# The first modulation columns from TensorE, and an affine step on ScalarE, in a two-block fp32 kernel

## The chip, the cores and the metric

One core of one Trainium2 chip runs the whole program. The metric is the device time of one execution in microseconds (us), the median of several runs. The engines are PE (TensorE; PEld is its weight load), DVE (VectorE), ACT (ScalarE), POOL (GpSimd) and SP (SyncE, which issues the DMAs here).

## The reference, cut to what matters

Two transformer-like blocks work on 512 tokens of 1024 channels in fp32. Only the very start of the first block is touched:

```python
mod = jax.nn.silu(c) @ w_ada[l] + b_ada[l]
shift1, scale1, gate1, shift2, scale2, gate2 = [m[:, None, :] for m in jnp.split(mod, 6, axis=-1)]
h = rms_norm(x, norm1_w[l]) * (1.0 + scale1) + shift1
proj = h @ w_in[l]
```

`c` is one row of 1024 numbers, `w_ada` is 1024 by 6144. Of the 48 columns of 128 outputs that `mod` has, column k is the shift and column 8 + k the scale of channel tile k (k = 0 to 7). What follows in the block (a state-space mixer, attention, a gated merge, an MLP) and the second block (a recurrence and latent attention) is as before.

## The kernel before

Channels lie on partitions, tokens along the free axis; a k tile is 128 channels by 512 tokens. Products in near-fp32 precision are made of three: each operand is split into a high part (fp32r, a copy on ACT) and a low part (the difference, on DVE or POOL), and `mm3` (L166) issues high by high, high by low, low by high. The profile gives these three lines as L168 to L170. `weight` (L143) loads a weight tile into the ring "wr" of four slots (DMA, L153), casts the high part on ACT (L156) and subtracts the low part on DVE or POOL by a counter (L159). `split` (L162) does the same for activations (L163 and L164).

The start runs like this. `setup` and `mod_setup` load the identity, the bias `b_ada` and the norms. `silu_c` (L328) loads c as one row, takes Tanh on ACT, multiplies on DVE, and spreads the row over 128 partitions with two native fp32 matmuls (L339) into `cs`, copied on ACT (L340). `norm1` (L346) loads x in four tiles, takes sums of squares on ACT (L293) with small steps on POOL, scales x on DVE (L356), transposes it tile by tile on PE (L362, 32 transposes) and copies eight tiles `xt` to SBUF on ACT (L365).

Then comes the k loop (L370). In each turn one of seven weight tiles is loaded and split (`FIRST`, while k < 7). `mod_tiles` (L252) loads two 512 KB tiles of `w_ada`, rows 8 + k and k, into the same ring "wr", and for each one DVE multiplies 128 x 1024 elements by `cs` and sums along the row into a column of `modc` (L257). DVE adds the bias (L377) and forms the gain column (L379), applies gain and shift to xt in place (L382), and the split of xt follows (ACT L163, POOL L164). With that k tile the products of four output tiles go on that have their weights. Those of the last three (`NX`) stand at k = 7 in the source. After the loop, the convolutions of the mixer begin (ACT L469, DVE L478); the dt product goes through a chain on DVE that ends in `av` (L436), which PE needs for a cumulative sum (L441).

The order on each engine is not that of the source. The framework under the kernel follows source order as a priority, and lets an instruction pass that it expects to be ready sooner. So products of the last three output tiles run from 37 us on in the trace. Slots of a ring (four in "wr", four banks in the PSUM pool "px") are given out in that order, and SP's queue, on which all these loads stand, serves its list in order: a load that waits for a slot holds up those behind it. `LO["start"]` and `PAD` are tuning constants: which weights' low parts go to POOL, and words of padding at the head of a stage's small tiles.

Of the kernel before, what the change touches and what calls it, by code (L numbers as in the profile page):

```python
# [6 lines left out]
F32 = mybir.dt.float32  # L7
F32R = mybir.dt.float32r
AF = mybir.ActivationFunctionType
ALU = mybir.AluOpType  # L10
# [7 lines left out]
NEG = -1.0e30  # L18
FIRST = [4, 5, 0, 1, -1, 2, 3]
NX = 3  # L20
NSSD = 19
NF = 14
NATT = 12
# [26 lines left out]
       "xb0": "gpsimd", "xb1": "vector", "rq0": "vector", "rq1": "vector", "rq2": "vector"}  # L50
AFF = [0, 2]
FB = [32, 0]
PAD = [0, 16, 56, 0, 32, 0, 32, 0, 0, 0, 56, 0, 48, 32, 0, 0, 0, 0, 0, 0]


def r32(ap):
# [3 lines left out]
class Build:  # L60
# [261 lines left out]
    def mod_setup(self):  # L322
# [2 lines left out]
        self.n1 = self.load("norm1_w", [128, 8])  # L325
        self.n2 = self.load("norm2_w", [128, 8])

    def silu_c(self):  # L328

        nc, a = self.nc, self.a  # L330
        c, th = [self.pool("wr").tile([128, 1024], F32, tag="wr", name=self.nm("c"))[0:1] for _ in range(2)]
        nc.sync.dma_start(out=c, in_=a["c"])
        nc.scalar.activation(out=th, in_=c, func=AF.Tanh, scale=0.5)
        nc.vector.scalar_tensor_tensor(out=c, in0=th, scalar=1.0, in1=c, op0=ALU.add, op1=ALU.mult)
        half = self.c([1, 128], "half")
        nc.vector.memset(half, 0.5)
        for i in range(2):
            p = self.ps()
            nc.tensor.matmul(p, lhsT=half, rhs=c[:, i * 512:i * 512 + 512], start=True, stop=True)  # L339
            nc.scalar.copy(out=self.cs[:, i * 512:i * 512 + 512], in_=p)  # L340
# [5 lines left out]
    def norm1(self):  # L346
        nc, a = self.nc, self.a
        rs = self.stats("r1")
        xb = self.big("x")
        xv = xb.rearrange("p a b -> p (a b)").rearrange("p (t d) -> p t d", t=NT)  # L350
        for t in range(NT):
            nc.sync.dma_start(out=xv[:, t], in_=a["x"][t])
        for t in range(NT):
            for b in range(2):
                self.half_stats(rs, xv[:, t, b * 512:b * 512 + 512], b, t)
            nc.vector.tensor_scalar(out=xv[:, t], in0=xv[:, t], scalar1=rs[2][:, t:t + 1], scalar2=None, op0=ALU.mult)  # L356
        self.g1 = self.c([128, 8], "g1")
        xts = []
        for k in range(8):
            p = self.ps()  # L360
            for t in range(NT):
                nc.tensor.transpose(out=p[:, t * 128:t * 128 + 128], in_=xv[:, t, k * 128:k * 128 + 128],  # L362
                                    identity=self.ident)
            xt = self.t("xt")
            nc.scalar.copy(out=xt, in_=p)  # L365
            xts.append(xt)
        n = len(FIRST)
        pss = [self.pm() if m < 4 else self.ps() for m in range(n)]
        ws = []
        for k in range(8):  # L370
            if k < n:
                i = FIRST[k]
                src = a["w_dt"][0] if i < 0 else a["w_xbc"][i if i < 4 else 16 + 4 * (i - 4)]
                ws.append(self.weight(src, own=k >= n - NX))
            self.mod_tiles([8 + k, k])
            j = slice(k, k + 9, 8)
            nc.vector.tensor_tensor(out=self.modc[:, j], in0=self.modc[:, j], in1=self.bada[:, j], op=ALU.add)  # L377
            g = self.g1[:, k:k + 1]
            nc.vector.scalar_tensor_tensor(out=g, in0=self.modc[:, 8 + k:9 + k], scalar=1.0, in1=self.n1[:, k:k + 1],  # L379
                                           op0=ALU.add, op1=ALU.mult)  # L380
            xt = xts[k]
            nc.vector.tensor_scalar(out=xt, in0=xt, scalar1=g, scalar2=self.modc[:, k:k + 1], op0=ALU.mult,  # L382
                                    op1=ALU.add)
            self.split(self.hh[:, k], self.hl[:, k], xt, eng=self.e("hsplit"))
            late = range(n - NX, n) if k == 7 else []
            for m, k1 in [(m, k1) for m in range(n - NX) for k1 in range(8) if max(m, k1) == k] + \
                    [(m, k1) for m in late for k1 in range(8)]:
                wh, wl = ws[m]
                self.mm3(pss[m][:wh.shape[2]], wh[:, k1], wl[:, k1], self.hh[:, k1], self.hl[:, k1], k1 == 0, k1 == 7)
        return pss  # L390
# [885 lines left out]
def emit(tc, a, out, dbg=None, stages=("b1", "b2")):  # L1276
    with ExitStack() as ctx:
        b = Build(tc, ctx, a, out, dbg)
        tail = ctx.enter_context(ExitStack())
        with b.phase(nw=NW), ExitStack() as inner:  # L1280
            b.setup()
            if "b1" in stages:
                b.mod_setup()
                with ExitStack() as A:
                    A.enter_context(b.phase(nbig=3))
                    b.cs = b.c([128, 1024], "cs")
                    cpool = b.pool("c")
                    big = lambda n, p=b.pool("big"): p.tile([128, 8, 512], F32R, tag="big", name=b.nm(n))
                    b.hh, b.hl, b.accS = b.big("hh", F32R), b.big("hl", F32R), b.big("accS")
                    with b.phase(nt=9, nbig=1, nx=2 * NX):  # L1290
                        b.lo_pool = LO["start"]
                        b.silu_c()
                        first = b.norm1()
                        b.cpool = cpool
                        b.ssd_setup()
                        b.cpool = None
                    A.enter_context(b.phase(nf=NF))
                    with b.phase(nt=NSSD):
                        b.lo_pool = LO["ssd"]
                        b.ssd(first)  # L1300
                    O = A.enter_context(ExitStack())
                    O.enter_context(b.phase(nbig=2))
                    b.oh, b.ol = b.big("oh", F32R), b.big("ol", F32R)
                    with b.phase(nt=NATT):
                        b.lo_pool = LO["attn"]
                        b.attention()
                    tail.enter_context(b.phase(nbig=1, side="right"))
                    b.lo_pool = LO["merge"]
                    b.residual_setup()
                    G = ExitStack()  # L1310
                    G.enter_context(b.phase(nt=3, side="right"))
                    b.gb = {j: b.c([128, 1024], f"gb{j}") for j in (16, 40)}
                    b.mh, b.ml = big("mh"), big("ml")
                    with b.fills():
                        b.merge()
                    b.mod_cols(16, 32)
                    b.gate_rows(16, 0.5)
                    b.gate_rows(40, 1.0)
                    b.out_proj()
# [30 lines left out]
def pack(i):  # L1350
# [4 lines left out]
    i = {k: np.asarray(v) for k, v in i.items()}  # L1355
    o = {}

    def cm(w):
        k, m = w.shape
        return w.reshape(k // 128, 128, m // 128, 128).transpose(2, 1, 0, 3)  # L1360
# [5 lines left out]
    def col(v):  # L1366
        return v.reshape(-1, 128).T

    o["x"] = i["x"].reshape(4, 128, 1024)
    o["c"] = i["c"].reshape(1, 1024)  # L1370
    o["w_ada"] = i["w_ada"][0].T.reshape(48, 128, 1024)
    o["b_ada"] = col(i["b_ada"][0])
    o["norm1_w"], o["norm2_w"] = col(i["norm1_w"][0]), col(i["norm2_w"][0])
# [87 lines left out]
```

## Time and profile before

| | us |
|---|---|
| median of 3 runs | 1675.04 (1671.86 to 1677.4) |
| the profiled execution | 1674.92 |
| its span, first to last instruction | 1673.1 |
| PE busy | 1591.9 (95%) |
| DVE busy | 1130.0 (68%) |
| ACT busy | 784.3 (47%) |
| POOL busy | 447.4 (27%) |

The profile is of one execution. Busy times are sums over an engine's instructions; a matmul's end is modelled, so that a busy PE may still have room. The rows in the section further down name a line of the kernel, an engine, the operation, the tiles written and read, and where an engine stood idle before, what released it.

### The profile page before, as it was taken

The numbers are of one execution on the slowest core, as the hardware profiler recorded it, in microseconds if no ns is written. First come the engines' busy times: TensorE is split into PE (matmuls) and PEld (weight loads), VectorE is DVE, ScalarE is ACT, GpSimd is POOL, SyncE is SP. The second block draws the span as 40 slices with busy tenths as digits, with TensorE's granted clock in tenths as the row PEclk, the third lists the DMA queues.
The fourth block names the chain that finished last, engine by engine and source line by source line (L and its number), as shares of the span: only waits on it lengthen the run. The fifth ranks groups of instructions, "written<-read, shape, count | busy, mean of one in ns | idle before, by whom it ended". The sixth has DMA issues, their size and how long they took to land. (4 is left out here: it accounts for less than half of the span.)

```text
span 1673.1 us, 20895 instructions
## 1 busy us (share of the span) xinstructions
PE 1591.9 (95%) x7696; PEld 1287.8 (77%) x7696; DVE 1130.0 (68%) x1948; ACT 784.3 (47%) x1511; POOL 447.4 (27%) x329
## 2 busy tenths in 40 slices
PE   5989999999999999999989999999989899999998
PEld 3767677677678778778879888888878777888886
DVE  7899689789869888973463343434457865757883
ACT  4357446354456666662353232323336562455552
POOL 3314345244353334321042020201131101521012
PEclk9999999999999999999999999999999999999999
DMA  7511223234223122225322233333313221322211
GB/s 257 187 53 62 63 76 127 63 101 134 78 63 101 57 83 88 87 74 177 93 76 88 89 101 100 91 99 101 101 52 114 78 79 52 100 78 67 67 64 51
DMA packets 50648, 153.54 MB, mean 92 GB/s; under 512 B 8177, under 2 KB 12913, under 8 KB 50546
## 3 DMA queue, kind: packets, MB, share of 16 engines
q1 hardware_dynamic: 50546, 152.22, 28.4%
q8 instruction: 60, 0.98, 0.2%
q14 instruction: 42, 0.34, 0.1%
HBM read 150.10 MB, written 2.10 MB: 91 GB/s over the span
## 5 line engine op out<-in xcount | busy, mean ns | idle before, releaser
L156 ACT CAST wh<-wr 128x1024 fp32r<-128x1024 f32 (+5 forms) x245 | 239.9, 980 | 417.7 <-PE pm L169 185.4
L159 DVE TENSOR_TENSOR wl<-wr,wh 128x1024 fp32r<-128x1024 f32 (+2 forms) x170 | 200.0, 1178 | 216.0 <-ACT wh L156 215.6
L159 POOL TENSOR_TENSOR wl<-wr,wh 128x1024 fp32r<-128x1024 f32 (+3 forms) x75 | 175.6, 2341 | 552.8 <-ACT wh L156 512.0
L168 PE MATMUL pm<-hh,wh 128*128 128x512 f32 x432 | 174.0, 407 | 8.5 <-ACT hh L163 6.8
L169 PE MATMUL pm<-hl,wh 128*128 128x512 f32 x432 | 175.5, 406 | 3.9 <-POOL hl L164 3.8
L170 PE MATMUL pm<-hh,wl 128*128 128x512 f32 x432 | 172.6, 400 | 0.0
L950 POOL TENSOR_TENSOR r<-r 128x512 f32<-128x512 f32 x32 | 50.8, 1589 | 260.1 <-ACT r L949 260.1
L168 PE MATMUL pm<-h,wh 128*128 128x512 f32 (+1 forms) x288 | 105.5, 368 | 0.0
L169 PE MATMUL pm<-h,wh 128*128 128x512 f32 (+1 forms) x288 | 105.4, 366 | 0.0
L170 PE MATMUL pm<-h,wl 128*128 128x512 f32 (+1 forms) x288 | 105.3, 366 | 0.0
L168 PEld LDWEIGHTS pm<-hh,wh 128*128 128x128 f32 x432 | 81.9, 190 | 30.2 <-ACT hh L163 8.3
L169 PEld LDWEIGHTS pm<-hl,wh 128*128 128x128 f32 x432 | 82.2, 190 | 26.9 <-POOL hl L164 7.2
L170 PE MATMUL pm<-wh,rl 128*128 128x512 f32 x256 | 99.6, 389 | 0.0
L168 PE MATMUL pm<-wh,rh 128*128 128x512 f32 x256 | 99.6, 389 | 0.0
L169 PE MATMUL pm<-wl,rh 128*128 128x512 f32 x256 | 99.6, 389 | 0.0
L731 POOL TENSOR_SCALAR pr<-pr,psum 128x512 f32<-128x512 f32 x64 | 64.6, 1021 | 128.8 <-DVE psum L727 70.7
L170 PEld LDWEIGHTS pm<-hh,wl 128*128 128x128 f32 x432 | 82.2, 190 | 19.7 <-issue 3.1
L478 DVE SCALAR_TENSOR_TENSOR acc<-pm,conv_w_s,acc 128x510 f32<-128x510 f32 (+2 forms) x118 | 87.7, 743 | 12.9 <-ACT acc L469 11.9
L614 POOL TENSOR_TENSOR e<-e,w 128x512 f32<-128x512 f32 x32 | 52.0, 1626 | 100.3 <-ACT e L613 85.9
L257 DVE SCALAR_TENSOR_TENSOR wada<-wada,cs 128x1024 f32<-128x1024 f32 x48 | 68.2, 1431 | 15.5 <-DMA wada<-in_w_ada 15.1
L726 ACT ACTIVATE pr<-px,nmax 128x512 f32<-128x512 f32 (+2 forms) x96 | 60.4, 637 | 29.9 <-DVE nmax L723 24.0
L168 PE MATMUL pm<-ha,wh 128*128 128x512 f32 (+1 forms) x192 | 69.0, 362 | 4.8 <-DVE acc L478 4.8
(401 smaller groups left out, 4138.3 us busy)
## 6 DMA issues: line engine op xcount, KB each, us to landing
wr<-in_w_mlp SPq DMA_DIRECT2D x64, 512.0 KB, 3.5
wada<-in_w_ada SPq DMA_DIRECT2D x48, 512.0 KB, 4.0
wr<-in_w_xbc SPq DMA_DIRECT2D x24, 512.0 KB, 3.5
wr<-in_w_in_a SPq DMA_DIRECT2D x20, 512.0 KB, 3.5
wr<-in_w_z SPq DMA_DIRECT2D x16, 512.0 KB, 3.6
wr<-in_w_ssd_out SPq DMA_DIRECT2D x16, 512.0 KB, 3.5
wr<-in_w_gate SPq DMA_DIRECT2D x16, 512.0 KB, 3.8
wr<-in_w_qkv SPq DMA_DIRECT2D x16, 384.0 KB, 3.0
```

What stands on the lines that cost most here:

```text
L156: nc.scalar.copy(out=hi[:, :n], in_=raw[:, :n])
L159: eng.tensor_tensor(out=lo[:, :n], in0=raw[:, :n], in1=r32(hi[:, :n]), op=ALU.subtract)
L168: m(out, lhsT=lh, rhs=rh, start=start, stop=False)
L169: m(out, lhsT=lh, rhs=rl, start=False, stop=False)
L170: m(out, lhsT=ll, rhs=rh, start=False, stop=stop)
L257: nc.vector.scalar_tensor_tensor(out=w, in0=w, scalar=1.0, in1=self.cs, op0=ALU.mult, op1=ALU.mult, accum_out=self.modc[:, j:j + 1])
L478: nc.vector.scalar_tensor_tensor(out=acc[:, lo:hi], in0=ps[:, lo + o:hi + o], scalar=w[:, j:j + 1], in1=acc[:, lo:hi], op0=ALU.mult, op1=A ...
L614: self.e("ew").tensor_tensor(out=e, in0=e, in1=w, op=ALU.mult)
L726: nc.scalar.activation(out=e[:, :n], in_=p, func=AF.Exp, bias=nmax, accum_out=s)
L731: self.e("norm").tensor_scalar(out=e[:, :n], in0=e[:, :n], scalar1=s, scalar2=1.0, op0=ALU.mult, op1=ALU.mult)
L950: self.e("sq").tensor_tensor(out=r, in0=r, in1=r, op=ALU.mult)
```

## The change

A new function `first_mods` stands between the loads of x and the first sums of squares, with `FM` = 2. It loads c as a 128 x 8 tile, forms silu(c) there (Tanh on ACT, two DVE steps on 8 columns), and for k = 0 and 1 and both scale and shift loads one 512 KB tile `w_ada_k` into a slot of its own (pool "q", four slots). Eight native fp32 matmuls per column, each with 128 x 128 of the weights as the stationary operand and one column of c as the moving one, add up a column in PSUM, and ACT adds the bias on its way to `modc`. In the k loop, k = 0 and 1 skip `mod_tiles` and the addition of the bias. For all eight tiles, the affine step on xt is an Identity activation on ACT with gain and shift as scale and bias instead of a DVE instruction. The padding of this stage shrinks by the 16 words that the two new small tiles take. The rows of `w_ada` for k = 0 and 1 are no longer read in their old form.

```diff
--- before.py
+++ after.py
@@ -18,6 +18,7 @@
 NEG = -1.0e30
 FIRST = [4, 5, 0, 1, -1, 2, 3]
 NX = 3
+FM = 2
 NSSD = 19
 NF = 14
 NATT = 12
@@ -50,7 +51,7 @@
        "xb0": "gpsimd", "xb1": "vector", "rq0": "vector", "rq1": "vector", "rq2": "vector"}
 AFF = [0, 2]
 FB = [32, 0]
-PAD = [0, 16, 56, 0, 32, 0, 32, 0, 0, 0, 56, 0, 48, 32, 0, 0, 0, 0, 0, 0]
+PAD = [0, 16, 40, 0, 32, 0, 32, 0, 0, 0, 56, 0, 48, 32, 0, 0, 0, 0, 0, 0]
 
 
 def r32(ap):
@@ -325,6 +326,24 @@
         self.n1 = self.load("norm1_w", [128, 8])
         self.n2 = self.load("norm2_w", [128, 8])
 
+    def first_mods(self, ks):
+
+        nc, a = self.nc, self.a
+        c, th = self.c([128, 8], "ccol"), self.c([128, 8], "cth")
+        nc.sync.dma_start(out=c, in_=a["c_col"])
+        nc.scalar.activation(out=th, in_=c, func=AF.Tanh, scale=0.5)
+        nc.vector.scalar_tensor_tensor(out=c, in0=th, scalar=1.0, in1=c, op0=ALU.add, op1=ALU.mult)
+        nc.vector.tensor_scalar(out=c, in0=c, scalar1=0.5, scalar2=None, op0=ALU.mult)
+        for k in range(ks):
+            for d in (8, 0):
+                w = self.pool("q").tile([128, 8, 128], F32, tag="q", name=self.nm("wak"))
+                nc.sync.dma_start(out=w, in_=a["w_ada_k"][k * 2 + (d == 0)])
+                p = self.ps((128, 1))
+                for i in range(8):
+                    nc.tensor.matmul(p, lhsT=w[:, i], rhs=c[:, i:i + 1], start=i == 0, stop=i == 7)
+                j = slice(k + d, k + d + 1)
+                nc.scalar.activation(out=self.modc[:, j], in_=p, func=AF.Identity, bias=self.bada[:, j])
+
     def silu_c(self):
 
         nc, a = self.nc, self.a
@@ -350,6 +369,7 @@
         xv = xb.rearrange("p a b -> p (a b)").rearrange("p (t d) -> p t d", t=NT)
         for t in range(NT):
             nc.sync.dma_start(out=xv[:, t], in_=a["x"][t])
+        self.first_mods(FM)
         for t in range(NT):
             for b in range(2):
                 self.half_stats(rs, xv[:, t, b * 512:b * 512 + 512], b, t)
@@ -372,15 +392,15 @@
                 i = FIRST[k]
                 src = a["w_dt"][0] if i < 0 else a["w_xbc"][i if i < 4 else 16 + 4 * (i - 4)]
                 ws.append(self.weight(src, own=k >= n - NX))
-            self.mod_tiles([8 + k, k])
-            j = slice(k, k + 9, 8)
-            nc.vector.tensor_tensor(out=self.modc[:, j], in0=self.modc[:, j], in1=self.bada[:, j], op=ALU.add)
+            if k >= FM:
+                self.mod_tiles([8 + k, k])
+                j = slice(k, k + 9, 8)
+                nc.vector.tensor_tensor(out=self.modc[:, j], in0=self.modc[:, j], in1=self.bada[:, j], op=ALU.add)
             g = self.g1[:, k:k + 1]
             nc.vector.scalar_tensor_tensor(out=g, in0=self.modc[:, 8 + k:9 + k], scalar=1.0, in1=self.n1[:, k:k + 1],
                                            op0=ALU.add, op1=ALU.mult)
             xt = xts[k]
-            nc.vector.tensor_scalar(out=xt, in0=xt, scalar1=g, scalar2=self.modc[:, k:k + 1], op0=ALU.mult,
-                                    op1=ALU.add)
+            nc.scalar.activation(out=xt, in_=xt, func=AF.Identity, scale=g, bias=self.modc[:, k:k + 1])
             self.split(self.hh[:, k], self.hl[:, k], xt, eng=self.e("hsplit"))
             late = range(n - NX, n) if k == 7 else []
             for m, k1 in [(m, k1) for m in range(n - NX) for k1 in range(8) if max(m, k1) == k] + \
@@ -1287,7 +1307,7 @@
                     cpool = b.pool("c")
                     big = lambda n, p=b.pool("big"): p.tile([128, 8, 512], F32R, tag="big", name=b.nm(n))
                     b.hh, b.hl, b.accS = b.big("hh", F32R), b.big("hl", F32R), b.big("accS")
-                    with b.phase(nt=9, nbig=1, nx=2 * NX):
+                    with b.phase(nt=9, nbig=1, nx=2 * NX, nq=2 * FM):
                         b.lo_pool = LO["start"]
                         b.silu_c()
                         first = b.norm1()
@@ -1368,6 +1388,8 @@
 
     o["x"] = i["x"].reshape(4, 128, 1024)
     o["c"] = i["c"].reshape(1, 1024)
+    o["c_col"] = col(i["c"].reshape(-1))
+    o["w_ada_k"] = cm(i["w_ada"][0])[[j for k in range(FM) for j in (8 + k, k)]]
     o["w_ada"] = i["w_ada"][0].T.reshape(48, 128, 1024)
     o["b_ada"] = col(i["b_ada"][0])
     o["norm1_w"], o["norm2_w"] = col(i["norm1_w"][0]), col(i["norm2_w"][0])
```

## Rows read from the trace of the kernel before

**Rows 1.** The page: span, PE's busy time, issues of the w_ada loads.

```profile
span 1673.1 us, 20895 instructions
...
PE 1591.9 (95%) x7696; PEld 1287.8 (77%) x7696; DVE 1130.0 (68%) x1948; ACT 784.3 (47%) x1511; POOL 447.4 (27%) x329
...
wada<-in_w_ada SPq DMA_DIRECT2D x48, 512.0 KB, 4.0
```

**Rows 2.** Windows by stage: stretch, length, busy us of each engine, clock, DMA.

```profile
core 0: us, PE busy (x) PEld busy (x) DVE busy (x) ACT busy (x) POOL busy (x), PEclk, DMA share, GB/s
...
10.00:15.00 5.00, 3.52 (x12) 2.07 (x12) 2.67 (x4) 3.84 (x11) 3.30 (x8) 1.00 0.97 391
...
20.00:60.00 40.00, 30.95 (x112) 21.06 (x113) 37.29 (x55) 9.10 (x13) 15.72 (x9) 0.91 0.76 246
...
64.00:96.00 32.00, 28.58 (x128) 22.73 (x126) 29.95 (x42) 12.89 (x18) 12.66 (x6) 0.99 0.34 107
```

**Rows 3.** Timeline, 12 to 21 us: start, duration, engine, line, idle before.

```profile
12.32 1.03 ACT L156 CAST wh<-wr 128x1024 fp32r<-128x1024 f32 x1
...
13.10 5.33 PE L362 MATMUL px<-ident,x 128*128 128x128 f32 x30 [1.07 <-DVE x L356]
...
14.51 1.22 DVE L159 TENSOR_TENSOR wl<-wr,wh 128x1024 fp32r<-128x1024 f32 x1
...
20.72 0.73 PE L168 MATMUL pm<-hh,wh 128*128 128x512 f32 x2 [2.29 <-ACT hh L163]
```

**Rows 4.** Timeline, 31 to 97 us.

```profile
31.53 0.55 DVE L382 TENSOR_SCALAR xt<-xt,g,modc 128x512 f32<-128x512 f32 x1
...
59.54 0.55 DVE L382 TENSOR_SCALAR xt<-xt,g,modc 128x512 f32<-128x512 f32 x1
...
62.99 0.78 ACT L469 ACTIVATE acc<-pm,conv_b_s,conv_w_s 128x512 f32<-128x512 f32 x1 [2.09 <-PE pm L170]
...
89.70 0.39 PE L169 MATMUL pm<-hl,wh 128*128 128x512 f32 x1
...
91.97 0.39 PE L170 MATMUL pm<-hh,wl 128*128 128x512 f32 x1
...
96.56 0.79 PE L441 MATMUL px<-av,k_tri_s 128*128 128x128 f32 x2 [3.98 <-DVE av L436]
```

**Rows 5.** Windows of PE alone: stretch, length, busy (count), clock, DMA.

```profile
28.50:33.80 5.30, 5.30 (x12) 0.50 0.74 260
...
20.70:92.60 71.90, 63.41 (x254) 0.95 0.60 196
```

**Rows 6.** Waits from 20 to 62 us: total, times, longest.

```profile
PE pm L168 <- ACT hh L163: 6.8, 3, 3.9
...
PE pm L169 <- POOL hl L164: 3.8, 5, 1.1
```

**Rows 7.** Groups on DVE from 14.4 to 60.8 us: busy us, mean ns.

```profile
L257 DVE SCALAR_TENSOR_TENSOR wada<-wada,cs 128x1024 f32<-128x1024 f32 x16 | 26.5, 1688 | 0.0
...
L382 DVE TENSOR_SCALAR xt<-xt,g,modc 128x512 f32<-128x512 f32 x8 | 4.4, 546 | 0.3
L377 DVE TENSOR_TENSOR modc<-modc,b_ada_s 128x2 f32<-128x2 f32 x8 | 3.3, 412 | 0.2
```

**Rows 8.** Groups on ACT in the first 70 us.

```profile
L156 ACT CAST wh<-wr 128x1024 fp32r<-128x1024 f32 x10 | 10.4, 1048 | 9.8 <-DMA wr<-in_w_xbc 9.8
L163 ACT CAST hh<-xt 128x512 fp32r<-128x512 f32 x8 | 5.0, 623 | 19.4 <-DVE xt L382 19.4
...
L414 ACT ACTIVATE acol<-acol 128x64 f32<-128x64 f32 x1 | 0.3, 252 | 0.0
```

**Rows 9.** Timeline of PE behind its stop: native matmuls, two instructions in each row.

```profile
97.14 0.63 PE L442 MATMUL px<-av,strict 128*128 128x128 f32 x2
97.57 1.06 PE L444 MATMUL px<-av,ones 128*128 128x256 f32 x2
```

**Rows 10.** Windows of the transposes alone (L362): PE, PEld, clock, DMA.

```profile
15.00:16.00 1.00, 1.00 (x7) 1.00 (x6) 1.00 0.01 4
...
17.00:18.00 1.00, 1.00 (x12) 1.00 (x10) 1.00 0.83 319
```

## The prediction

> **What bounds the kernel now.** The execution that I work from lasts 1674.92 us, 1.82 us around its span of 1673.1; the median of the three timed runs, 1675.04 us, is 0.12 us above it, so a difference in the span goes straight onto the median. The page comes first: PE is busy 95% of the span [rows 1]. A share over 1673 us says little on the first 100, which are all that this change touches, so the next view is the windows by stage. From 20 to 60 us DVE is busy 37.29 of 40 us, PE 30.95; from 64 to 96 us DVE is busy 29.95 of 32 [rows 2]. The start is therefore a chain on DVE, with PE close behind.
>
> The timeline names its links. The transposes of x occupy PE from 13.10 to 18.43 us, the first product runs at 20.72 [rows 3]. The k loop then needs until 59.54 for the eighth tile, although the third came at 31.53. Right after the eighth the first convolution opens at 62.99; from there DVE works without a pause towards the cumulative sum of the dt product, for which PE stops 3.98 us and goes on at 96.56 [rows 4]. What the change is worth is how much earlier that restart comes: behind it PE is nearly full and takes a shift of everything ahead of it along.
>
> PE's side of the same stretch: from 20.7 to 92.6 us it issues 254 matmuls, 4 of them small transposes [rows 5]. Full products follow each other every 0.227 us (ten steps from 89.70 to 91.97) [rows 4]; 250 of them are 56.8 us of the 71.9. The rest: 6.8 and 3.8 us of waits for hh and hl [rows 6]; 12 products at a granted clock of 0.50, 1.2 of 2.4 GHz, 5.3 us where 2.7 would do, so 2.6 lost [rows 5]; 1.9 us of small things.
>
> **The change, part by part.**
>
> 1. *DVE loses work.* Four modulation products of 1.69 us mean, 6.8 us; two additions of the bias, 0.41 us mean, 0.8; eight affine steps of 0.546, 4.4 [rows 7]. Together 12.0 us of the 46 that end with the eighth tile. Added to DVE: two operations on 8 columns, at most 0.41 us each by the additions of the bias, in the gap that the later first weight opens on DVE (part 2). The mean of the products contains slow ones; were all four as fast as a weight's low part, 1.22 us [rows 3], I would lose 1.9 us of the term.
>
> 2. *Loads change places.* Four tiles of 512 KB and one small one stand on SP's queue ahead of the first weight, in slots of their own, and four go out behind it. From 10 to 15 us the transfers run at 391 GB/s [rows 2], so 524 KB cost 1.34 us, four 5.4. The first weight, cast at 12.32 us now [rows 3], is there at about 17.7, its low part at 20.0 (1.03 us of cast, 1.22 of DVE). The next on the queue land at 1.34 us each: weights two and three by 20.4, the first tile of w_ada for k=2 by 21.7; its second needs the ring slot that the first weight leaves at 20.0, and lands 4.0 us after its issue, the median of these loads [rows 1]. So k=2 is modulated at about 26 rather than 31.53 [rows 4], 5.5 us earlier. Five more tiles save 0.55 us of affine step each on DVE, 2.7 in all. The eighth tile, and the dense DVE chain behind it, come 8.2 us earlier.
>
> 3. *The affine step on ACT.* 512 columns on ACT take 0.62 us, as the cast of hh does, against 0.546 on DVE [rows 7, 8]. The cast of hh stands right behind it on the same engine and saves the hop from DVE. ACT is busy 9.1 of the 40 us [rows 2], so 8 x 0.62 = 5.0 us fit. I cost it at nothing; without that cover it is 0.07 us a tile.
>
> 4. *PE gets 32 native matmuls of one column*, two passes each as every native one here: 64 pairs of weight load and matmul, ahead of the transposes in source order. No row has one column. The nearest are native pairs of 128 columns right behind PE's stop, two in 0.43 us (97.14 to 97.57), 0.215 each [rows 9], and transposes, whose load is also 128 columns wide: 7 in the microsecond from 15 us, 12 in the one from 17 [rows 10]. The clock column has 1.00 for both; the rates say that PE ran nearer to half speed in the first. So 64 pairs cost between 64/12 = 5.3 us and 64 x 0.215 = 13.8; I take the transposes' earlier rate, 64/7 = 9.1, as the work next to it at the same point of the kernel. The tiles land from 12.3 us, where the first weight is now, to 16.3; PE starts at 12.3 and has 9.1 us of this and 32/7 = 4.6 of transposes: the products begin at some 26 us instead of 20.72. The row says that a narrow matmul still pays for a wide load, whatever it streams. The Trainium skill (TensorE: Matmul & The Clock Gate, section "LDWEIGHTS (loading the stationary operand)") states this as a rule: a load's time goes by its columns, 128/1.2 = 107 ns. By that rule the estimate would be 64 x 0.107 = 6.8 us and the products would begin at 23.7; the trace's nearest rows have 0.083 to 0.215 us a pair, either side of it.
>
> 5. *Small parts.* Four one-column ACT operations and a short Tanh, 0.25 us each by the nearest row [rows 8], wait for PE's columns; behind the last of them on ACT may stand casts of weights and of hh. Whether they stand there is the planner's choice, between 0 and about 6 us for weight two (from 19 us to 25); I take nothing, since the landing times leave DVE waiting for k=2 until 24, and keep the 6 for a rival.
>
> **The sum.** Two ends meet at the restart of PE. DVE's: 96.56 less 8.2 gives 88.4. PE's: 26 + 56.8 + 2.6 + 1.9, and 2 us of waits left of 10.6 since it now has a backlog, gives 89.3. The later one counts, a gain of 7.3 us. Rounded to 7, 0.4%: from 1674.92 to 1668 us, and the same against the median.
>
> **The rivals.**
>
> *The cover is gone: no change.* The columns come slowly, ACT's casts stand behind the last of them, and the ring of four slots fills late. If weight two is cast at 25 us, its slot frees at 27, and the tile of k=3 lands after 31; the eighth tile then gains 2 us from the shorter DVE steps and nothing else. For it: ACT works its list off in order, and 9.8 us of its waits in the first 70 us are for weights [rows 8], so their lateness shows. Against it: the planner placed the casts of weights among other work by when they land. 1673 us, within 0.3%, which is 5.0 us and about what a measurement of this kernel can tell from no change.
>
> *PE becomes the bound: slower.* At 0.215 us a pair [rows 9] and with the transposes at their slower rate throughout [rows 10], columns and transposes end at 30.7; if PE then starts the products at the lower clock, they cost 0.44 instead of 0.227 us [rows 5], and 6 us of them lose 3. Casts behind the last column begin near 28, k=2 comes at 36.5 rather than 31.5, and 2.7 are won back: +2.3 at the eighth tile, +3 for the clock: 5.3 us. It decides from the point at which a pair costs over 0.2 us and the weights' casts queue behind the columns. 1680 us.
>
> *The change doesn't reach the chain.* The planner could order the columns after the transposes; then the first two tiles come no earlier, only the 4.4 us of affine steps and part of the products remain: 1671 us, within 0.3%.
>
> **How the numbers follow.** The forecast's case, gains of 4 to 11 us, gets 0.50; 0.40 of it lie beyond 5 us. No change gets 0.27, of that 0.01 beyond 5 us; the columns after the transposes 0.08, of that 0.02. Slower by over 5 us gets 0.12 for the bound on PE, and 0.03 for shifts of order later in the program, which no row prices. Faster 0.43, same 0.42, slower 0.15. The range takes the forecast's own, 1664 to 1671, and reaches up over the no-change case to 1679: the loads' rate and a warm pair (4 us less on PE) give its lower end, the half-clock case cut at the top its upper.
>
> **What would show it.** Right: no DVE work on k=0 and k=1 but the gain column; PE's 64 narrow pairs in 7 to 11 us, done by 26; the first weight cast near 17.7; k=2 modulated near 26, the eighth tile near 51; PE's restart for the cumulative sum near 89; from there the same rows, 7 us earlier. Wrong: narrow pairs over 0.2 us; ACT idle behind a column while weights lie ready; an eighth tile later than 57 us; or a shift at the restart that a later wait takes back.

## The result, and the profile after

The changed kernel takes 1691.41 us (median of 4 runs, 1688.38 to 1695.84) against 1674.38 us of the kernel before (4 runs, 1671.86 to 1677.4): ratio 1.0105, 95% interval 1.0088 to 1.0123, 17.0 us slower. The prediction had 1668 us and a range up to 1679. The profiled execution took 1695.84 us around a span of 1694.0; it is the slowest of the four, so its shifts near the end are some us larger than those of the median.

The page of the changed kernel, its span and busy times, against [rows 1]:

```profile
span 1694.0 us, 21024 instructions
...
PE 1609.3 (95%) x7760; PEld 1304.0 (77%) x7760; DVE 1123.6 (66%) x1932; ACT 791.3 (47%) x1524; POOL 446.7 (26%) x329
```

DVE has lost 6.4 us of work and PE has gained 17.4, of which the columns are 13.8. Most of what happened is in the first 37 us. The timeline of that stretch, against [rows 3] (line numbers have moved: L157 is the cast that was L156, L169 the product that was L168, L382 the transposes; L343 is new):

```profile
13.26 13.81 PE L343 MATMUL px<-ccol,wak 128*128 128x1 f32 x64 [2.94 <-DVE ccol L336]
16.87 0.26 ACT L345 ACTIVATE modc<-px,b_ada_s 128x1 f32<-128x1 f32 x1 [3.90 <-PE px L343]
...
26.93 5.45 PE L382 MATMUL px<-ident,x 128*128 128x128 f32 x32
27.11 0.26 ACT L345 ACTIVATE modc<-px,b_ada_s 128x1 f32<-128x1 f32 x1 [3.15 <-PE px L343]
...
30.62 2.54 ACT L385 COPY xt<-px 128x512 f32<-128x512 f32 x5 [0.27 <-PE px L382]
33.02 1.08 ACT L157 CAST wh<-wr 128x1024 fp32r<-128x1024 f32 x1
33.97 0.85 ACT L403 ACTIVATE xt<-xt,modc,g 128x512 f32<-128x512 f32 x1
34.13 1.23 DVE L160 TENSOR_TENSOR wl<-wr,wh 128x1024 fp32r<-128x1024 f32 x1 [9.99 <-ACT wh L157]
35.39 0.33 SPq L257 DMA_DIRECT2D wada<-in_w_ada  x1
36.32 0.49 PE L169 MATMUL pm<-hh,wh 128*128 128x512 f32 x1 [3.94 <-ACT hh L164]
```

Read it from the top. PE forms the four columns from 13.26 to 27.07 us, 0.215 us a pair. All 32 transposes stand behind them. ACT, which works its list in order, waits for each column, then copies eight tiles xt, and only then casts the first weight: at 33.02 us, 12.32 before [rows 3]. The low part follows, a slot of the ring comes free at 35.36, and at 35.39 SP issues the w_ada load that was waiting for it. The first product comes 15.6 us later than before. Of these, 13.95 are PE's own list, whose transposes end at 32.38 us instead of 18.43 [rows 3]; the rest is a longer wait for ACT, 3.94 us instead of 2.29.

The same windows as in [rows 2] and [rows 5] show that DVE starves now:

```profile
20.00:60.00 40.00, 30.85 (x135) 24.81 (x135) 23.67 (x30) 18.02 (x28) 12.78 (x7) 0.96 0.51 159
...
36.30:108.90 72.60, 64.37 (x260) 48.23 (x260) 62.62 (x90) 29.25 (x40) 31.05 (x16) 0.95 0.55 179
```

DVE is busy 23.67 of the 40 us in which it had 37.29 [rows 2]. The second line is the stretch from the first product to PE's restart: 72.6 us, where the kernel before has 96.56 - 20.72 = 75.8 [rows 3, 4]. PE is busy 64.37 us of it (63.41 before [rows 5]) and in both kernels waits some 8 us besides the stop at its end; what it saves is that stop. The timeline around the restart, and behind it:

```profile
69.57 0.81 ACT L403 ACTIVATE xt<-xt,modc,g 128x512 f32<-128x512 f32 x1 [1.46 <-DVE g L400]
73.96 0.77 ACT L489 ACTIVATE acc<-pm,conv_b_s,conv_w_s 128x512 f32<-128x512 f32 x1
...
108.96 0.49 PE L461 MATMUL px<-av,k_tri_s 128*128 128x128 f32 x2 [0.34 <-DVE av L456]
...
117.29 2.35 POOL L160 TENSOR_TENSOR wl<-wr,wh 128x1024 fp32r<-128x1024 f32 x1 [8.67 <-ACT wh L157]
118.37 1.81 DVE L587 TENSOR_TENSOR xw<-xtm,tk 128x512 f32<-128x512 f32 x1
120.32 2.05 PE L589 MATMUL px<-xw,Btm 128*128 128x512 f32 x2 [4.51 <-DVE xw L587]
```

The eighth tile is 10.0 us late, the first convolution 11.0, the restart 12.4: PE waits 0.34 us for av instead of 3.98 [rows 4], so 15.6 less 3.6. That accounts for 12 of the 17 us. The rest arises behind the restart. What first shows there is that PE stops 4.51 us, up to 120.32, for DVE's first xw; the kernel before has no such stop there.

### The profile page after: what moved, and what is told of

Same layout as the page of the kernel before. It is cut to its first block, busy times and chain, and to the rows that moved or that the text cites. A ratio compares the mean times of both kernels' runs of the same rounds, so it can differ in the third digit from the quotient of the medians.

```text
span 1694.0 us, 21024 instructions
## 1 busy us (share of the span) xinstructions
PE 1609.3 (95%) x7760; PEld 1304.0 (77%) x7760; DVE 1123.6 (66%) x1932; ACT 791.3 (47%) x1524; POOL 446.7 (26%) x329
## 5 line engine op out<-in xcount | busy, mean ns | idle before, releaser
L157 ACT CAST wh<-wr 128x1024 fp32r<-128x1024 f32 (+5 forms) x245 | 239.7, 980 | 417.7 <-PE pm L170 191.8
L169 PE MATMUL pm<-hh,wh 128*128 128x512 f32 x432 | 173.9, 406 | 4.7 <-ACT hh L164 3.9
L169 PE MATMUL pm<-h,wh 128*128 128x512 f32 (+1 forms) x288 | 106.2, 371 | 0.0
L169 PEld LDWEIGHTS pm<-hh,wh 128*128 128x128 f32 x432 | 82.2, 190 | 26.5 <-ACT hh L164 4.4
L169 PE MATMUL pm<-wh,rh 128*128 128x512 f32 x256 | 99.6, 389 | 0.0
L169 PE MATMUL pm<-ha,wh 128*128 128x512 f32 (+1 forms) x192 | 69.3, 364 | 4.8 <-DVE acc L498 4.8
L258 DVE SCALAR_TENSOR_TENSOR wada<-wada,cs 128x1024 f32<-128x1024 f32 x44 | 59.6, 1357 | 19.7 <-DMA wada<-in_w_ada 17.7
```

The costliest lines, as they stand in the source:

```text
L157: nc.scalar.copy(out=hi[:, :n], in_=raw[:, :n])
L169: m(out, lhsT=lh, rhs=rh, start=start, stop=False)
L258: nc.vector.scalar_tensor_tensor(out=w, in0=w, scalar=1.0, in1=self.cs, op0=ALU.mult, op1=ALU.mult, accum_out=self.modc[:, j:j + 1])
```

## The experiments

The kernel before ran beside every call (medians 1673.0 to 1674.4 us); each ratio below is against those runs. The table gives how much later than in the kernel before four points come in the profiled execution: the first convolution (62.99 us before), PE's restart (96.56), the first square of the mixer's output (149.09), the last Tanh of the convolutions (402.8). The profiled execution is one of the 4 to 11 behind a median and lies up to 4.6 us off it (e15: 1679.8 us, the changed kernel: 1695.8), so these columns need not add up to the time.

| run | time, us | ratio [95%] | conv | restart | 149 | 403 |
|---|---|---|---|---|---|---|
| after | 1691.4 | 1.0105 [1.0088, 1.0123] | +11.0 | +12.4 | +15.0 | +17.7 |
| e1 affine only | 1682.0 | 1.0053 [1.0034, 1.0072] | -3.2 | -0.1 | +4.1 | +6.3 |
| e2 columns only | 1694.6 | 1.0131 [1.0111, 1.0152] | +12.2 | +14.8 | +17.0 | +18.6 |
| e3 32 pairs | 1684.8 | 1.0069 [1.0048, 1.0089] | +4.9 | +6.3 | +9.0 | +9.1 |
| e4 8 pairs | 1679.4 | 1.0034 [1.0018, 1.0050] | +1.6 | +3.3 | +7.1 | +5.6 |
| e5 behind transposes | 1694.9 | 1.0123 [1.0101, 1.0146] | +11.4 | +14.8 | +18.0 | +19.1 |
| e6 k = 6, 7 in the loop | 1685.1 | 1.0077 [1.0057, 1.0098] | +9.3 | +12.7 | +9.3 | +7.3 |
| e7 e1, two low parts exchanged | 1678.3 | 1.0029 [1.0018, 1.0040] | -2.8 | +0.3 | +0.4 | +2.6 |
| e8 affine, four tiles | 1672.6 | 0.9993 [0.9983, 1.0002] | -3.3 | -2.9 | -2.4 | -2.1 |
| e9 after, exchanged | 1697.8 | 1.0147 [1.0134, 1.0161] | +12.4 | +13.8 | +18.7 | +21.6 |
| e10 after, wide passes | 1681.8 | 1.0061 [1.0039, 1.0082] | +1.8 | +3.2 | +6.4 | +7.0 |
| e11 e8 again | 1672.9 | 1.0001 [0.9992, 1.0009] | -3.1 | -2.7 | -2.7 | -2.8 |
| e12 k = 0 ahead of x | 1692.1 | 1.0112 [1.0096, 1.0127] | +6.5 | +7.1 | +9.6 | +16.4 |
| e13 e6, wide passes | 1685.6 | 1.0061 [1.0043, 1.0079] | +5.9 | +8.6 | +5.3 | +7.5 |
| e14 e10, exchanged | 1685.5 | 1.0057 [1.0037, 1.0076] | +1.1 | +2.8 | +4.4 | +8.4 |
| e15 e10, affine four | 1684.4 | 1.0057 [1.0040, 1.0074] | +1.9 | +3.3 | +4.3 | +4.5 |

### The parts alone, and fewer pairs (e1 to e4)

Three theories stand against each other. P: what costs is PE's time for the 64 narrow pairs ahead of the first product. A: it is the affine step on ACT. L: it is the new order of the loads on SP's queue.

e1: the kernel before with this part of the change alone.

```diff
-            nc.vector.tensor_scalar(out=xt, in0=xt, scalar1=g, scalar2=self.modc[:, k:k + 1], op0=ALU.mult,
-                                    op1=ALU.add)
+            nc.scalar.activation(out=xt, in_=xt, func=AF.Identity, scale=g, bias=self.modc[:, k:k + 1])
```

> The kernel before with the affine step on ACT and nothing else of the change. Theory P (what costs is PE's time on 64 narrow pairs ahead of the first product): there are no pairs here, DVE is relieved of 8 x 0.546 us, ACT takes 8 x 0.82 instead; first product within 1 us of 20.7, restart for the cumulative sum at 94 to 98, 1671 to 1677 us. Theory A (the affine step on ACT and what queues behind it costs): most of the 17 us is here, 1685 to 1692.

e2: the changed kernel with the same two lines turned round, the affine step back on DVE.

> The changed kernel with the affine step back on DVE. P: the pairs are all there, the first product stays near 36 us, 1688 to 1694 us. A: the loss goes away, 1672 to 1678.

e3 and e4: fewer pairs for each column; the rest of the sum over the channels of c is left out.

```diff
-                for i in range(8):
-                    nc.tensor.matmul(p, lhsT=w[:, i], rhs=c[:, i:i + 1], start=i == 0, stop=i == 7)
+                for i in range(4):
+                    nc.tensor.matmul(p, lhsT=w[:, i], rhs=c[:, i:i + 1], start=i == 0, stop=i == 3)
```

> The changed kernel with 4 of the 8 matmuls per column; half of the sum over c is left out of the first two tiles' modulation. Loads, ACT steps and DVE work are as in the changed kernel. P: pairs take 6.9 instead of 13.8 us, the first product runs near 30 us instead of 36.3, the restart comes 5 to 7 us earlier than 109, 1683 to 1687 us. Theory L (the four tiles ahead of the first weight delay the k loop, whatever PE does): as the changed kernel, 1689 to 1693.

e4 has `range(1)` and `stop=i == 0` in their place.

> The changed kernel with 1 of the 8 matmuls per column; seven eighths of the sum are left out. P: pairs take 2 us, columns wait for the loads only, the first product runs near 25 us and the restart near 94 to 97, 1672 to 1678 us; if the sum of the prediction was right but for the pairs, the restart comes before 92 and the time is 1666 to 1670. L: 1687 to 1693.

With 64, 32 and 8 pairs the time is 1691.4, 1684.8 and 1679.4 us while every load stands where the change put it, and the first convolution is late by 11.0, 4.9 and 1.6 us. So the loads' new order is not the main cause; the pairs' time is. (With 8 pairs the first product still comes at 27.23 us, 6.5 late: its lateness is not passed on whole.) e2 shows that the columns alone bring the whole loss. e1 was not foreseen: the start is 3.2 us earlier, as it should be, but the time is 8 us longer. Its timeline behind the start:

```profile
93.73 2.40 POOL L159 TENSOR_TENSOR wl<-wr,wh 128x1024 fp32r<-128x1024 f32 x1 [10.61 <-ACT wh L156]
94.51 1.90 DVE L435 SCALAR_TENSOR_TENSOR av<-tk,acol 128x256 f32<-128x256 f32 x1
...
96.47 0.79 PE L440 MATMUL px<-av,k_tri_s 128*128 128x128 f32 x2 [5.94 <-DVE av L435]
...
106.46 2.34 POOL L159 TENSOR_TENSOR wl<-wr,wh 128x1024 fp32r<-128x1024 f32 x1 [10.33 <-ACT wh L156]
107.35 2.00 DVE L566 TENSOR_TENSOR xw<-xtm,tk 128x512 f32<-128x512 f32 x1
109.50 1.46 PE L568 MATMUL px<-xw,Btm 128*128 128x512 f32 x2 [4.00 <-DVE xw L566]
```

Both av and xw run while POOL subtracts a weight's low part, and last 1.90 and 2.00 us; av took 0.42 in the kernel before, and the median of the 24 xw in this trace is 0.68. PE stops 5.94 us for av, 3.98 before [rows 4], and 4.00 us for xw. A window on the 3.4 us behind that stop has a granted clock of 0.51.

### Where the columns stand (e5, e6)

e5 moves one line of the changed kernel.

```diff
             nc.sync.dma_start(out=xv[:, t], in_=a["x"][t])
-        self.first_mods(FM)
...
             xts.append(xt)
+        self.first_mods(FM)
```

> Edit: the changed kernel, but with the call that forms the four columns on TensorE standing behind the transposes of x in the source instead of ahead of them. Theory P (the 13.7 us that PE spends on 64 narrow pairs stand ahead of the first product wherever they are put): the transposes end near 18 us as in the kernel before, the columns fill about 18 to 32 us, the first product comes at 33 to 35 us, and the time stays at 1687 to 1692 us. Rival O (what costs is that transposes, copies of xt and casts of weights are queued behind the columns): the casts of weights run by 20 us, the third tile and the w_ada loads come as early as before, and the time falls to 1677 to 1682 us.

The transposes end at 19 us and the first product still comes at 33.31; the time is 1694.9 us, 3 over P's range. O is not settled, because its sign, casts by 20 us, did not come. The two columns that the first tile needs are in `modc` at 23.57 us, but ACT waits for the two of k = 1 before it casts a weight:

```profile
23.31 0.26 ACT L345 ACTIVATE modc<-px,b_ada_s 128x1 f32<-128x1 f32 x1 [2.16 <-PE px L343]
26.73 0.26 ACT L345 ACTIVATE modc<-px,b_ada_s 128x1 f32<-128x1 f32 x1 [3.15 <-PE px L343]
30.14 0.26 ACT L345 ACTIVATE modc<-px,b_ada_s 128x1 f32<-128x1 f32 x1 [3.15 <-PE px L343]
...
31.71 1.03 ACT L157 CAST wh<-wr 128x1024 fp32r<-128x1024 f32 x1
```

What falls is that the transposes and copies of xt behind the columns are the cost. No run here parts PE's time for the columns from the casts that wait behind them on ACT. The windows of the narrow matmuls alone (length, PE, PEld, clock, DMA) show more:

```profile
19.00:21.00 2.00, 1.99 (x19) 2.00 (x19) 1.00 0.51 205
21.00:23.00 2.00, 2.00 (x15) 2.00 (x14) 0.71 0.00 0
23.00:25.00 2.00, 2.00 (x11) 2.00 (x11) 0.50 0.04 8
```

Behind the transposes the pairs begin at 0.105 us each. While PE issues nothing else, the granted clock falls to 0.50 (1.2 of 2.4 GHz), and the last two columns, 16 pairs each, come 3.41 us apart: 0.213 a pair, the price that the changed kernel pays throughout.

e6 forms the columns of k = 6 and 7 from a call at k = 3 of the loop; the affine step is on DVE.

```diff
...
+            if k == 3:
+                self.first_mods(FM)
-            if k >= FM:
+            if k < 8 - FM:
...
```

> Edit: the four columns of k = 6 and 7 (not 0 and 1) are formed on TensorE, from a call at k = 3 of the loop, and the affine step stays on VectorE. The same 64 pairs then run among products, with PE at work before them. If a pair costs 0.215 us there too, PE loses 13.8 us in a stretch where it is busy three quarters of the time: no gain or a loss, 1675 to 1682 us. If a pair costs near 0.11 us, as a rate of the transposes at the higher clock would have it, the columns cost 7 us that fit into PE's gaps, DVE is rid of four products (6.8 us) and the eighth tile comes 4 to 6 us earlier: 1668 to 1672 us.

A miss on both sides: the two halves of 32 pairs take 3.63 and 3.69 us, 0.113 to 0.115 a pair, and yet the time is 1685.1 us and the eighth tile 2.1 us late. The timeline says why:

```profile
34.04 14.61 SPq L257 DMA_DIRECT2D wada<-in_w_ada  x2
...
37.38 3.63 PE L343 MATMUL px<-ccol,wak 128*128 128x1 f32 x32
39.26 0.26 ACT L345 ACTIVATE modc<-px,b_ada_s 128x1 f32<-128x1 f32 x1 [5.61 <-PE px L343]
...
42.59 3.69 PE L343 MATMUL px<-ccol,wak 128*128 128x1 f32 x32
```

ACT waits 5.61 us for a column with casts behind it, the ring stays full, and the second of two w_ada loads goes out 14 us behind the first. From 50 to 60 us the granted clock is 0.52, where the kernel before has 1.00.

### The affine step: a collision, or an order? (e7, e8, e9, e11)

e7 is e1 with the low parts of two neighbouring weights exchanged between POOL and DVE; e9 does the same to the changed kernel.

```diff
-        eng = nc.gpsimd if (self.lo_n * self.lo_pool) % 12 < self.lo_pool else nc.vector
+        q = {15: 16, 16: 15}.get(self.lo_n, self.lo_n)
+        eng = nc.gpsimd if (q * self.lo_pool) % 12 < self.lo_pool else nc.vector
```

> Edit: the kernel before with only the affine step on ScalarE, and the engines of the low parts of two neighbouring weights of the mixer's stage exchanged, so that POOL has no subtraction at the moment at which DVE forms the first xw. Theory D (DVE's first xw lasted 2.0 instead of 0.7 us because it ran beside POOL's subtraction, PE stopped 4.0 us for it and then ran at the lower clock): xw lasts 0.7 us, the stop at the first state product shrinks to 2.7 us or less, and the time falls from 1682 to 1677 to 1679 us. Rival E (the order of the engines behind the start is what costs, the collision is a bystander): the xw is short but the time stays within 1 us of 1682 us.

e8 is the kernel before with both forms of the step:

```diff
+            if k < 4:
+                nc.scalar.activation(out=xt, in_=xt, func=AF.Identity, scale=g, bias=self.modc[:, k:k + 1])
+            else:
+                nc.vector.tensor_scalar(out=xt, in0=xt, scalar1=g, scalar2=self.modc[:, k:k + 1], op0=ALU.mult,
+                                        op1=ALU.add)
```

> Edit: the kernel before with the affine step on ScalarE for the first four tiles alone. In the planned order DVE's first xw then stands behind the same instructions as in the kernel before. Theory E (the loss of the affine step on ScalarE comes from another order of DVE and PE behind 96 us): the loss of 8 us is gone altogether, 1671 to 1676 us. Rival F (each affine step on ScalarE costs by itself, 0.82 us against 0.55 on VectorE, and by what queues behind it): half of the loss stays, 1677 to 1679 us.

In e7 the timeline has the xw short and the stop of PE shorter by as much, and the window behind it has a granted clock of 1.00:

```profile
107.57 0.68 DVE L567 TENSOR_TENSOR xw<-xtm,tk 128x512 f32<-128x512 f32 x1
108.40 1.10 PE L569 MATMUL px<-xw,Btm 128*128 128x512 f32 x2 [2.69 <-DVE xw L567]
...
108.40:115.00 6.60, 6.60 (x23) 4.19 (x24) 6.32 (x9) 2.87 (x5) 0.00 (x0) 1.00 0.24 82
```

The time is 1678.3 us, as D has it. In e8 the whole loss of e1 is gone, as E has it: F falls, since four steps on ACT cost nothing. In its waits of PE from 86 to 200 us xw does not appear at all; the stop there is that of the kernel before, 1.7 us for acc:

```profile
PE px L444 <- DVE av L439: 4.4, 1, 4.4
PE pm L168 <- DVE acc L481: 1.7, 1, 1.7
```

> Edit: the changed kernel, with the low parts of the same two neighbouring weights exchanged between POOL and VectorE as in the run before with the affine step alone. Theory D (the changed kernel also pays for DVE's first xw beside POOL's subtraction, 1.81 us at 118.4 us, with a PE stop of 4.5 us and a spell at the lower clock behind it): xw takes 0.7 us, the stop shrinks to 3.3 us or less, and the time falls by 2 to 5 us, to 1686 to 1689 us. Rival: the start is 11 us later here, so other collisions take its place and the time stays at 1690 to 1693 us.

> The kernel before with the affine step on ScalarE for the first four tiles alone, once more and with more rounds. Theory E has the 2.8 us of the start kept to the end: 1671 to 1673 us, 0.1% to 0.2% under the kernel before. Rival: the difference was chance, and the ratio lies within 0.05% of one.

In e9 the xw, the stop and the window behind it (all engines, as in [rows 2]) are these:

```profile
119.79 0.68 DVE L588 TENSOR_TENSOR xw<-xtm,tk 128x512 f32<-128x512 f32 x1
120.62 2.04 PE L590 MATMUL px<-xw,Btm 128*128 128x512 f32 x2 [3.38 <-DVE xw L588]
...
120.50:127.30 6.80, 6.27 (x9) 2.67 (x9) 5.01 (x8) 2.27 (x4) 0.00 (x0) 0.50 0.24 77
```

e9 refutes D for the changed kernel: xw takes 0.68 us there, the stop shrinks from 4.5 to 3.4, but a lower-clock spell of 6.8 us follows as before and the time is 1697.8 us, 6 more. e11 repeats e8 and finds no gain in the median (1.0001), though its profiled span keeps 2.8 us up to 403 us. So e8 is no better than the kernel before, within 0.1%.

### Wide passes (e10, e12)

e10: each pass streams the column 128 times, and ACT reads the first result.

```diff
...
-                p = self.ps((128, 1))
+                p = self.ps((128, 128))
...
-                    nc.tensor.matmul(p, lhsT=w[:, i], rhs=c[:, i:i + 1], start=i == 0, stop=i == 7)
+                    nc.tensor.matmul(p, lhsT=w[:, i], rhs=c[:, i:i + 1].to_broadcast([128, 128]), start=i == 0, stop=i == 7)
...
```

> Edit: the changed kernel, but each of the 64 passes streams 128 columns (the one column of c repeated) instead of one. Theory W (a one-column pass leaves the clock low and the price of 0.215 us is a price of the lower clock; wide passes raise it as the transposes do): the first passes take 0.215 us, the later ones 0.11 us, the columns take 8 to 10 us instead of 13.7, transposes and products behind them start at the higher clock, and the time falls to 1684 to 1688 us. Rival N (the price belongs to the pair, whatever the clock, and columns streamed come on top): the columns take 13.7 us or more and the time is 1691 to 1696 us.

W holds, and by more than it said: 9.6 us faster than the changed kernel. The timeline, to be read against the first one of the changed kernel:

```profile
13.35 9.14 PE L343 MATMUL px<-ccol,wak 128*128 128x128 f32 x64 [3.14 <-DVE ccol L336]
...
20.91 1.03 ACT L157 CAST wh<-wr 128x1024 fp32r<-128x1024 f32 x1
...
22.33 3.65 PE L382 MATMUL px<-ident,x 128*128 128x128 f32 x32
...
28.10 2.12 SPq L257 DMA_DIRECT2D wada<-in_w_ada  x2
```

64 passes of 128 columns take 9.14 us, 64 of one column 13.81. The first column of 16 pairs is read 3.8 us behind PE's start, the others follow 1.79 us apart, 0.112 a pair. The transposes behind take 3.65 us instead of 5.45. Together 6.5 us; the cast of the first weight is placed between two columns at 20.91, so the ring empties earlier and the first product comes at 29.18.

e12: the columns of k = 0 alone, c and their weights loaded ahead of x by a function of their own, the affine step as in e8.

```diff
-FM = 2
+FM = 1
...
+        self.first_loads(FM)
+        self.first_mods(FM)
         for t in range(NT):
             nc.sync.dma_start(out=xv[:, t], in_=a["x"][t])
-        self.first_mods(FM)
...
```

> Edit: the changed kernel with the columns of k = 0 alone (32 pairs), their weights and c loaded ahead of x, and the affine step on ScalarE for the first four tiles alone. Theory P (what the columns cost is PE time ahead of the transposes, 0.215 us a pair): PE forms them while it waits for x; x comes 2 to 3 us later, the transposes end near 21 us, DVE is rid of two products and four affine steps, and the eighth tile comes 0 to 3 us earlier than in the kernel before: 1670 to 1676 us. Rival: columns and the casts behind them still hold up the first product by the 6.9 us of 32 pairs: 1678 to 1683 us.

A miss: 1692.1 us. 32 pairs take 6.99 us, and the timeline shows what they hold up:

```profile
17.16 0.26 ACT L354 ACTIVATE modc<-px,b_ada_s 128x1 f32<-128x1 f32 x1 [3.15 <-PE px L352]
17.32 0.62 ACT L294 ACTIVATE sqj<-x 128x512 f32<-128x512 f32 x1
```

The squares of the last two tiles of x stand on ACT behind the second column. That explains the first product at 29.07 and +6.5 us at the convolution, which is as far as the rival goes; another 9 us arise between the restart and 403 us, most of them behind 149 us (see the windows below).

### What was left open (e13 to e15)

e13 is e6 with the edit of e10, e14 is e10 with the edit of e7, e15 is e10 with the edit of e8.

> Edit: as in the run with the columns of k = 6 and 7 formed from k = 3 of the loop and the affine step on VectorE, but each pass streams 128 columns. Theory W (narrow passes let the clock fall, and the products behind them ran at half of it from 46 to 59 us): the clock stays at the higher level, 64 passes take 7 to 9 us, the first convolution opens 5 to 9 us earlier than with narrow passes, and the time is 1674 to 1679 us. Rival Q (the columns' place in the queues of PE and ScalarE is what costs): no change against the narrow passes, 1682 to 1687 us.

> Edit: the run with wide passes, with the low parts of the two neighbouring weights exchanged between POOL and VectorE. Theory D (the collision of DVE's first xw with POOL's subtraction, 1.67 us at 109.2 us, makes the stop of 4.2 us and the spell at the lower clock): xw takes 0.7 us, the stop is under 3 us, no spell at the lower clock follows, and the time falls by 3 to 4 us to 1678 to 1679 us. Rival E (the order behind the start costs, as in the changed kernel with the same exchange): the time stays within 1.5 us of 1682 us, or rises.

> Edit: the run with wide passes, with the affine step on ScalarE for the first four tiles alone. If the affine step's place is the second cause by itself, 1674 to 1677 us. If it is the order that it happens to bring (the planned order here has the first xw where the run with the affine step alone had it), the later loss of 5 us stays: 1679 to 1683 us.

The columns of e13 on PE:

```profile
37.47 7.31 PE L343 MATMUL px<-ccol,wak 128*128 128x128 f32 x64
```

e13: its 64 wide pairs take 7.31 us, as W had it, but so do the 64 narrow ones of e6 (3.63 and 3.69 us). The first convolution comes 3.4 us earlier than in e6 and the second w_ada load waits 9 us instead of 14, yet the time is the same, 1685.6 us, in Q's range. That a column's place in ACT's and SP's queues is what costs is argued, not shown: from 50 to 60 us the granted clock is 0.69, so W's condition came only in part.

e14: xw is 0.68 us, the stop still 3.16, a window on the 6.8 us from 108.6 has a granted clock of 0.50, and the time is 1685.5, not 1678 to 1679: D falls here too.

e15: its profiled execution has a stop of 4.15 us at xw, as e10 has. The median of 1684.4 us lies above both branches, and its eight executions fall apart, three from 1678.6 to 1679.8 and five from 1684.1 to 1688.5. The first branch falls, and four steps on ACT instead of eight bring no gain here; that the order is the reason, as the second branch has it, is not shown.

What stays open: why one order of DVE and PE behind the start costs 5 us more than another. From the restart to 149 us the runs change by -3.4 (e6) to +4.9 us (e9), from 149 to 403 by -2.0 (e6) to +6.8 (e12), with the same work there. The granted clock explains part of it. These are the windows of PE (length, PE, clock, DMA) from the third to the fourth point, in the kernel before, in e6 and in e12:

```profile
149.10:402.80 253.70, 244.09 (x1150) 0.99 0.28 88
...
158.40:410.10 251.70, 241.24 (x1144) 1.00 0.28 88
...
158.70:419.20 260.50, 248.73 (x1143) 0.97 0.27 85
```

In steps of 2 us the lower clock adds up to 3.4, 0 and 17 us there. If half of it is lost, that is an estimate of 1.7 us less in e6 and 6.8 more in e12, nearly their whole shifts. From the restart to 149 us e6 and e13 have none of the 5.6 us of the kernel before, 2.8 of the 3.4 and 3.3 us that they win. The rest has no such rule: the changed kernel, e7, e9 and e13 lose 2 to 3 us from 149 to 403 at the clock of the kernel before, and why the spells come in one order and not in another is not shown. None of the versions beats the kernel before.

## Why the prediction was wrong

**Part 1, DVE loses work: right, and worth nothing.** DVE has 12 products left instead of 16, and the affine steps are gone. But it is busy 23.67 of 40 us: it waits for ACT and for loads. The argument that the start is a chain on DVE [rows 2] held for the kernel before alone.

**Part 2, loads change places: failed at the cast.** The first weight was to be cast near 17.7 us, when it lands; it is cast at 33.02, because ACT's list has the columns and eight copies of xt first. So k = 2 gets its affine step at 43.96 us, not near 26, and the eighth tile is 10.0 us later instead of 8.2 earlier.

**Part 3, the affine step at nothing: failed twice.** It lasts 824 ns a tile, not the 620 of the cast of hh:

```profile
L403 ACT ACTIVATE xt<-xt,modc,g 128x512 f32<-128x512 f32 x8 | 6.6, 824 | 16.6 <-DVE g L400 16.6
```

The Trainium skill (ScalarE: Activation LUTs, section "What ACT_TABLE_LOAD costs") has a price for this: 186 ns and 0.833 ns a column, and about 93 ns for each operand of scale or bias that is read from a tile. For 512 columns and two such operands the estimate by that page is 0.80 us; the trace agrees. At the start the longer step did no harm (e1: 3.2 us gained, 4.4 forecast). What it cost came behind 93 us: e1 ends 8 us later than the kernel before. The prediction gave shifts of order 0.03 and no price.

**Part 4, the pairs: the mis-sized term.** 9.1 us was taken between ends of 5.3 and 13.8; it is 13.81, the upper end, the price of [rows 9]. The transposes' earlier rate [rows 10] was the wrong neighbour: it is an average over a rise of the clock, which wide passes bring (e10: 9.14 us, almost what was forecast) and the narrow ones did not. The transposes behind them then cost 5.45 us, not 4.6. That a narrow matmul pays for its wide load was read from rows without a narrow one; e6 and e13 bear it out, 0.113 us a pair with one column and 0.114 with 128. By the page quoted there (the Trainium skill, TensorE: Matmul & The Clock Gate, section "LDWEIGHTS (loading the stationary operand)") the estimate was 0.107 us a load; the 0.113 a pair of e6, at the higher clock, agrees, and the changed kernel paid twice that.

**Part 5, casts behind the last column: taken as 0, kept as 0 to 6.** They are there, with eight copies besides, and the range was too small.

**The sum.** PE's end was the later one, as forecast, but at 108.96 us and not at 89.3. Of the difference, 10.3 us are the first product (36.32, not 26), 6.2 the waits behind it (8.2, not 2) and 3.1 PE's busy time (64.4, not 61.3). The hope that a backlog would swallow the waits was wrong: PE still waits 5.2 us for hl, 2.0 for dtx and 1.1 for a weight and av. The waits of 10.6 us for the kernel before were themselves 2.3 too many, because 2.29 of the 6.8 for hh end at 20.72, where the stretch begins [rows 3, 6]; PE is busy 63.41 us in it [rows 5].

**The rivals.** "PE becomes the bound" is what happened, and its point of decision was right: pairs over 0.2 us, casts queued behind the columns. It had columns and transposes end at 30.7 us; they end at 32.4. What it got wrong is the price, 5.3 us: it carried the loss through the eighth tile, where PE's whole list moves by 15.6 us and gets back only 3.6 of the stop of 3.98. It should have given 12 us, and more chance than 0.12, because the row nearest in form, a native pair behind a stop, stood at its condition. "The columns after the transposes" would not have saved the change (e5).

## What to carry to other kernels

A new operation on an engine that works in order is priced by everything that its list holds back: here the columns on PE moved the transposes by 14 us, and four small ACT steps that wait for PE held up the casts, the ring of buffers, and with it the loads. Take the price of a small matmul from the row with the same state of the clock. Where the clock is low and one column is wanted, try a wide pass: it was 4.7 us cheaper for 64 pairs in e10, and no cheaper at the higher clock (e13 against e6). When a planner orders the engines, a change of the start moves everything behind it: between two points with the same work the runs here win up to 3.4 and lose up to 6.8 us, part of it by the clock. Measure a small gain with the order that it brings.

## What the runs showed of the hardware

More columns can cost less time: 64 native pairs took 9.14 us with 128 columns (e10) and 13.81 with one, in the same place. With one column the granted clock fell from 1.00 to 0.50 while PE issued them without a gap (e5). At 1.00 the two widths cost the same, 7.31 us for 64 pairs with 128 columns (e13) and 3.63 for 32 with one (e6). The clock column is no proof at a program's start: from 13.26 to 27.00 us the changed kernel has 1.00 there, but its columns come 3.41 us apart, the spacing that e5 has at 0.50.

A DVE operation that reads two tiles of SBUF is held up beside a POOL subtraction: xw took 2.00 us at 107.35 in e1 with POOL busy from 106.46 to 108.80, and 0.68 without. A convolution step at 106.69, whose input is in PSUM, took its usual 0.74 beside the same subtraction. The Trainium skill (GPSIMD Engine Reference, section "1. Specifications") says that POOL shares its SBUF interfaces with VectorE and contends with DVE instructions that have two SBUF inputs; these rows agree. Taking that collision away saved 3.8 us in one kernel (e7) and nothing in two (e9, e14).
